# The room of the split weights holds four more expert tiles: a ring of eleven, and the turn of twice the slots at place 20

## The chip, the cores and the metric

One Trainium2 chip, and one of its cores. The metric is the device time of one execution in microseconds (us). The kernel before takes 2090.07 us, the median of three runs.

## The reference

Two transformer-like blocks on 256 tokens of width 1024, in f32. What matters here is the feed-forward part of the first block, a mixture of 32 experts:

```
logits = xt @ w_router + b_router
top_val, top_idx = lax.top_k(logits, 4)          # 4 of 32 experts for each of 256 tokens
hcat = xb @ w_in[e] + b_in[e]                    # 1024 -> 2048
act  = min(hcat[:, :1024], 7) * sigmoid(1.702 * .) * (clip(hcat[:, 1024:]) + 1)
y    = act @ w_out[e] + b_out[e]                 # 1024 -> 1024, added to the token by its gate
```

Ahead of it, in the first block, come the projections and two kinds of attention (the last four heads of the second kind are called "d" below) and a modulation vector that is made from the matrix `ada_w`. Behind it comes a second block: a retention part, convolutions, a state-space part and two more feed-forward parts.

## The kernel before

All large weights come from HBM as tiles of [128 x 2048] f32 (1 MB; those of `ada_w` are 0.5 MB) through one queue, that of SyncE (SP). The class `Stream` keeps the list of their sources in the order of use. `issue` asks for the next tile as long as the tile whose buffer it takes has been used; `ahead` asks for one tile out of turn, into a pool that is named.

The list begins with nine tiles of the projections (0 to 8) and four of the attention's output (9 to 12). From 13 on there are 12 for each of the 32 turns of the experts: eight of `w_in` and four of `w_out`; the first two turns interleave them, so that 13 to 28 are the `w_in` of turns 0 and 1 and 29 to 32 the `w_out` of turn 0. The experts end with tile 396.

In the other parts of the kernel a weight is not used as it comes. `Parts` splits each half of a tile in two numbers of fewer bits, `hi` (ScalarE, L141) and `lo` (VectorE, L142), and TensorE multiplies by both. Their buffers are the pool `wsplit`: four of `hi` and four of `lo`, 32 KB of each partition. The weights of the experts are not split, so `wsplit` holds nothing from the last projection to the end of the experts.

The ring of the tiles is `wst` (four buffers) with `mw` (three more), which exists while the experts run: seven tiles from tile 25 on. Tiles 13 to 24 are asked for during the attention, into `wst`, `mw` and two other pools (`hw`, `hx`).

Turns 0 and 1 have a fixed expert each. The later turns take their experts by the number of tokens, from a table `turn` that VectorE makes once the router is done; SP reads a turn's expert from it (TENSOR_LOAD, L1917) before it asks for the turn's tiles. An expert's tokens are gathered into slots: 64 for a turn, and 128 for the one turn `WIDE`, which takes the expert with the most tokens. For a 64-slot turn the two column halves of a product lie in the two row halves of one bank, and the profile shows the matmuls as 128*64; for the wide turn each half has a bank of its own and 128 rows, shown as 128*128 (`products`, L918). Gather is L900, transposes of the activations L947, scatter L1007.

On the engines the instructions stand in the order that a scheduler has given them; SP's queue is served in the order of issue.

Of the kernel before, what the change touches and what calls it, by code (L numbers as in the profile page):

```python
# [8 lines left out]
F32 = mybir.dt.float32  # L9
F32R = mybir.dt.float32r  # L10
# [8 lines left out]
NSTAGE = 4  # L19
# [18 lines left out]
AHEAD = 2  # L38
# [2 lines left out]


FIXED = 2
WIDE = 4
SLOTS = 64
S5W = 2816
INV2PI = 0.15915494309189535
# [19 lines left out]
class Stream:  # L67
# [2 lines left out]

    def __init__(self, nc, pool, n, width, late=None):
        self.nc, self.pool, self.n, self.width, self.late = nc, pool, n, width, late
        self.sources, self.tiles, self.more = [], {}, None
        self.issued = self.at = 0
        self.held = {}

    def add(self, srcs):
        self.sources += srcs

    def extend(self, pool, n, first, last):  # L80

        self.more = (pool, n, first, last)

    def ahead(self, i, pool):

# [3 lines left out]
    def issue(self, done):  # L89

        while self.issued < len(self.sources):
            i, pool, n = self.issued, self.pool, self.n
            if i in self.tiles:
                self.issued += 1
                continue
            if self.more and self.more[2] <= i < self.more[3] and (i - self.more[2]) % (self.n + self.more[1]) >= self.n:
                pool, n = self.more[:2]
            held = self.held.setdefault(id(pool), [])
            if len(held) >= n and held[-n] >= done:
                break  # L100
            held.append(i)
            self.load(i, pool.tile([128, self.width], F32, tag="w", name="w"))
            self.issued += 1
# [8 lines left out]
    def get(self):  # L112
        self.issue(self.at)
        self.at += 1
        return self.tiles.pop(self.at - 1)


class Parts:
# [7 lines left out]
    def get(self):  # L126
        st = self.stream
        end = 2 * len(st.sources)
        while self.ready < min(self.at + AHEAD + 1, end):
            i, h = divmod(self.ready, 2)  # L130
            if h == 0:
                st.issue(i)
                self.raw = st.tiles.pop(i)
            w = self.raw[:, h * 1024:(h + 1) * 1024]
            if self.ready in self.whole:
                self.made[self.ready] = (w,)
                self.ready += 1
                continue
            hi = self.pool.tile([128, 1024], F32R, tag="hi", name="hi")
            lo = self.pool.tile([128, 1024], F32R, tag="lo", name="lo")  # L140
            self.nc.scalar.copy(out=hi, in_=w)  # L141
            self.nc.vector.tensor_tensor(out=lo, in0=w, in1=hi.bitcast(F32), op=ALU.subtract)  # L142
            self.made[self.ready] = (hi, lo)
            self.ready += 1
        st.issue(self.ready // 2)
        self.at += 1
        return self.made.pop(self.at - 1)
# [146 lines left out]
def attention_block(tc, g):  # L294

    nc, A, ws = tc.nc, g.A, g.ws
    v, s, pe = nc.vector, nc.scalar, nc.tensor
    xT1 = g.xT1
    with ExitStack() as es:
# [135 lines left out]
        slots = [0, len(todo)]  # L435

        def ada_step(n=1):

            slots[0] += n
            for _ in range(min(len(todo) - slots[1] + slots[1] * slots[0] // ADA_PLACES, len(todo))):  # L440
                with tc.high_priority(offset=-LOW1):
                    todo.pop(0).step((lambda: bank1("s")) if todo else None)
# [79 lines left out]
        def stage_scores(heads, i):  # L522
            kind, c, j = heads[i]
            out = []
            for qt in range(2):
                qs = slice(qt * 128, (qt + 1) * 128)
                if kind == "g":
                    r = slice(64 * j, 64 * j + 64)
                    p, z = soft(scores(qT[r, c, qs], kaT[r, :], kind))
                    s.activation(out=p, in_=p, func=ACTF.Copy, scale=z)  # L530
                else:
                    pz = []
                    for m in range(2):
                        pz.append(soft(scores(qd[:, c, m, qs], kbT[:, c], kind)))
                    (p, z), (p1, z1) = pz
                    v.tensor_tensor(out=z1, in0=z1, in1=nlam, op=ALU.mult)
                    v.tensor_scalar(out=p, in0=p, scalar1=z, scalar2=None, op0=ALU.mult)
                    v.scalar_tensor_tensor(out=p, in0=p1, scalar=z1, in1=p, op0=ALU.mult, op1=ALU.add)
                out.append(p)
            pend[i] = out  # L540

        def stage_T(heads, i):
            pT = at.tile([128, 4, 256], F32, tag="pTs", name="pTs")
            for qt, p in enumerate(pend[i]):
                transposed(p, pT, qt)
            pend[i] = pT

        def stage_pv(heads, i):
            kind, c, j = heads[i]
            pT = pend.pop(i)  # L550
            o = bank1("o" if kind == "g" or c % 2 == 0 else "sc")
            if kind == "g":

                for k in range(4):
                    pe.matmul(out=o[:64, :256], lhsT=va[:, k, 64 * j:64 * j + 64], rhs=pT[:, k], start=(k == 0), stop=(k == 3))
                r = slice(64 * j, 64 * j + 64)
                s.copy(out=mix[r, c], in_=o[:64, :256])
            else:
                for k in range(4):
                    pe.matmul(out=o[:, :256], lhsT=vd[:, k, 128 * c:128 * c + 128], rhs=pT[:, k], start=(k == 0), stop=(k == 3))  # L560
                o2, osb = (o24[:, c % 2, j] for j in range(2))
                s.activation(out=o2, in_=o[:, :256], func=ACTF.Square)
                s.activation(out=osb, in_=o[:, :256], func=ACTF.Copy, scale=g.subln)
                for t in range(2):
                    pe.matmul(out=o[:, 256 + t:257 + t], lhsT=o2[:, t * 128:(t + 1) * 128], rhs=g.ones[:, :1], start=True, stop=True)
                r = rsqrt(nc, at, o[:, 256:258], 2, 1.0 / 128, "d", v)
                spread(g, at, r, o[:, 256:])
                v.tensor_tensor(out=mix[:, 4 + c], in0=osb, in1=o[:, 256:], op=ALU.mult)

        def attend(heads):  # L570
            n = len(heads)
            for i in range(n + 2):
                if i < n:
                    stage_scores(heads, i)
                if 0 <= i - 1 < n:
                    stage_T(heads, i - 1)
                if 0 <= i - 2 < n:
                    stage_pv(heads, i - 2)
                ada_step(2 if i % 2 else 1)
# [84 lines left out]
        for i in range(20, 24, 2):  # L664
            t = g.hw.tile([128, 2, 2048], F32, tag="h", name="hw")
            for j in range(2):
                ws.stream.load(i + j, t[:, j])
        attend([("d", h, 0) for h in range(4)])
        for i in (17, 18, 24):
            ws.stream.ahead(i, g.mw)  # L670
        ws.stream.extend(g.mw, 3, 25, 13 + 32 * 12 - 1)
        es_a.close()
        o1 = es.enter_context(tc.tile_pool(name="o1", bufs=1))
        sq, xs = (o1.tile([128, 8, 256], F32, name=n) for n in ("sq1", "xs"))
# [17 lines left out]
        first = pe.matmul(out=acc[:, :66], lhsT=g.ones[:1], rhs=g.zero, start=True, stop=False)  # L692
# [15 lines left out]
        last = tc.keep_in_program_order(chunk(7))  # L708
# [72 lines left out]
def turns(tc, g, mp, rp):  # L781
# [12 lines left out]
    jk = rp.tile([128, 32], F32, name="jk")  # L794
    v.tensor_scalar(out=jk, in0=g.iota[:, :32], scalar1=-1.0, scalar2=float(WIDE), op0=ALU.mult, op1=ALU.add)
    v.tensor_tensor(out=jk, in0=jk, in1=oh, op=ALU.mult)
    v.tensor_tensor(out=jk, in0=jk, in1=g.iota[:, :32], op=ALU.add)
    v.tensor_copy(out=jk[:, WIDE:WIDE + 1], in_=fx[:, 0:1])
    g.turn = mp.tile([128, 32], I32, name="turn")
# [3 lines left out]
    for t in range(2):  # L803
        for src, dst in ((g.rk, g.rkt), (g.gate, g.gatet)):
            sx = rp.tile([128, 1], F32, tag="sx", name="sx")
            v.scalar_tensor_tensor(out=jk, in0=src[:, t], scalar=1.0, in1=oh, op0=ALU.mult, op1=ALU.mult, accum_out=sx)
            v.scalar_tensor_tensor(out=jk, in0=src[:, t], scalar=src[:, t, WIDE:WIDE + 1], in1=oh, op0=ALU.subtract, op1=ALU.mult)
            v.tensor_tensor(out=dst[:, t], in0=src[:, t], in1=jk, op=ALU.subtract)
            v.tensor_copy(out=dst[:, t, WIDE:WIDE + 1], in_=sx)


def turn_biases(tc, g, rp):
# [6 lines left out]
    v.tensor_reduce(out=binx, in_=bx.rearrange("p e c -> p c e"), axis=AX.X, op=ALU.add)  # L819
    v.tensor_tensor(out=bx, in0=g.binT, in1=bc(g.binT[:, WIDE], 1, 32), op=ALU.subtract)  # L820
    v.tensor_tensor(out=bx, in0=bx, in1=bc(oh, 2, 16), op=ALU.mult)
    v.tensor_tensor(out=g.binT, in0=g.binT, in1=bx, op=ALU.subtract)
    v.tensor_copy(out=g.binT[:, WIDE], in_=binx)

# [1287 lines left out]
```

## Time and profile before

| | before |
|---|---|
| median of 3 runs | 2090.07 us (2088.04 to 2090.89) |
| the profiled execution | 2090.91 us, span 2089.2 us |
| TensorE busy | 1951.1 us, 93% |
| VectorE, ScalarE busy | 54%, 31% |
| queue of the weights | 613.46 MB, 75.1% of the span on 16 DMA engines |
| tiles' issue to landing, `w_in` | 13.1 us (median) |
| tiles' issue to landing, `ffn_up` (second block) | 5.0 us (median) |

The share of a span is a mean over stages: TensorE is the busier engine in the whole, but the row of GB/s shows a long flat part in the middle. A profile's row of slices cuts the span in 40 equal pieces; a window is a stretch that one chooses. A busy TensorE can hold small waits, since the ends of its matmuls are modelled.

### The profile page before, as it was taken

To read this page: it belongs to the slowest core of one execution; us is meant where nothing else is said; L and a number is where in the kernel's file an instruction comes from. 1 tells how busy PE (TensorE), PEld (TensorE's weight loads), DVE (VectorE), ACT (ScalarE), POOL (GpSimd) and SP (SyncE) were. 2 spreads that over 40 slices of the span, in tenths; PEclk is the share of its full clock that TensorE was granted. 3 is DMA by queue.
4 is the path that set the end of the run, shared out by engine and by line. 5 is a ranking of instruction groups with operands and counts; after the bars stand their busy time and mean duration, and the time that the engine had idled before them with its cause. 6 is when DMAs were issued, how large, how long until landed. Compare 5 with 4: busy or idle time off the path is not lost. (4 is left out here: it accounts for less than half of the span.)

```text
span 2089.2 us, 29010 instructions
## 1 busy us (share of the span) xinstructions
PE 1951.1 (93%) x11166; PEld 1246.5 (60%) x11166; DVE 1125.1 (54%) x2378; ACT 648.0 (31%) x1135; POOL 59.2 (3%) x92
## 2 busy tenths in 40 slices
PE   6999989999999989999998997999999999899998
PEld 3856844444333333332333326888999999599998
DVE  5865765132222212221222127999898978768863
ACT  3464311000000000000000004446677645256542
POOL 0000000000000000000000000000001002100000
PEclk9999989999999999999999998999999999799999
DMA  8656559999999999999999994667857778655651
GB/s 315 223 162 221 207 224 365 405 379 375 421 421 421 421 421 420 422 421 421 421 421 421 421 414 160 228 221 273 301 213 249 271 286 296 211 186 192 223 182 61
DMA packets 101757, 643.40 MB, mean 308 GB/s; under 512 B 11584, under 2 KB 12880, under 8 KB 34288
## 3 DMA queue, kind: packets, MB, share of 16 engines
q1 hardware_dynamic: 94176, 613.46, 75.1%
q0 software_dynamic: 6624, 26.76, 3.8%
q8 instruction: 89, 1.46, 0.3%
q10 hardware_dynamic: 816, 1.30, 0.2%
q14 instruction: 52, 0.43, 0.1%
HBM read 626.79 MB, written 14.68 MB: 307 GB/s over the span
## 5 line engine op out<-in xcount | busy, mean ns | idle before, releaser
L918 PE MATMUL hc<-w,xe 128*64 128x512 f32 (+1 forms) x2008 | 476.1, 598 | 54.1 <-DMA w<-in_w_in_dram 54.0
L918 PEld LDWEIGHTS hc<-w,xe 128*64 128x64 f32 (+1 forms) x2008 | 142.4, 138 | 375.3 <-issue 218.4
L142 DVE TENSOR_TENSOR lo<-w,hi 128x1024 fp32r<-128x1024 f32 x238 | 289.1, 1219 | 75.0 <-ACT hi L141 74.0
L141 ACT CAST hi<-w 128x1024 fp32r<-128x1024 f32 x238 | 249.0, 1049 | 253.0 <-PE b L241 156.7
L240 PE MATMUL b<-h2h,hi 128*128 128x256 f32 x896 | 254.6, 285 | 10.7 <-ACT h2h L1729 9.1
L938 DVE COPY hs<-hc 128x512 f32<-128x512 f32 x33 | 22.8, 691 | 448.8 <-PE hc L918 448.8
L241 PE MATMUL b<-h2l,hi 128*128 128x256 f32 x896 | 254.5, 285 | 0.2
L242 PE MATMUL b<-h2h,lo 128*128 128x256 f32 x896 | 253.9, 284 | 0.0
L918 PE MATMUL yb<-w,hb 128*64 128x512 f32 (+1 forms) x1024 | 252.6, 604 | 0.5 <-DMA w<-in_w_out_dram 0.5
L240 PEld LDWEIGHTS b<-h2h,hi 128*128 128x128 f32 x896 | 169.8, 190 | 13.3 <-ACT h2h L1729 9.3
L241 PEld LDWEIGHTS b<-h2l,hi 128*128 128x128 f32 x896 | 169.7, 190 | 4.0 <-issue 1.1
L242 PEld LDWEIGHTS b<-h2h,lo 128*128 128x128 f32 x896 | 169.7, 190 | 0.4 <-issue 0.4
L936 ACT COPY hs<-hc 128x512 f32<-128x512 f32 x33 | 19.3, 585 | 464.2 <-PE hc L918 464.2
L918 PEld LDWEIGHTS yb<-w,hb 128*64 128x64 f32 (+1 forms) x1024 | 66.8, 137 | 127.5 <-issue 119.5
L192 DVE SCALAR_TENSOR_TENSOR acc<-w,c,acc 128x1024 f32<-128x1024 f32 x77 | 98.4, 1278 | 12.0 <-DMA w<-in_ada_w_dram 11.4
L240 PE MATMUL b<-ah,hi 128*128 128x256 f32 x352 | 100.3, 286 | 0.0
L242 PE MATMUL b<-ah,lo 128*128 128x256 f32 x352 | 99.9, 284 | 0.2 <-DVE lo L142 0.2
L241 PE MATMUL b<-al,hi 128*128 128x256 f32 x352 | 99.4, 283 | 0.0
L981 ACT COPY ys<-yb 64x512 f32<-64x512 f32 (+1 forms) x32 | 18.5, 578 | 243.1 <-PE yb L918 243.1
L900 PEld LDWEIGHTS gb<-S,h 128*128 128x128 f32 x544 | 66.7, 197 | 37.2 <-issue 25.8
L1009 DVE TENSOR_TENSOR yacc<-sc,yacc 128x512 f32<-128x512 f32 x68 | 46.7, 688 | 66.5 <-PE sc L1007 66.5
L900 PE MATMUL gb<-S,h 128*128 128x128 f32 (+1 forms) x544 | 74.9, 289 | 1.2 <-DVE S L891 1.2
(523 smaller groups left out, 3061.1 us busy)
## 6 DMA issues: line engine op xcount, KB each, us to landing
w<-in_w_in_dram SPq DMA_DIRECT2D x252, 1024.0 KB, 13.1
w<-in_w_out_dram SPq DMA_DIRECT2D x128, 1024.0 KB, 14.5
w<-in_ffn_up_dram SPq DMA_DIRECT2D x44, 1024.0 KB, 5.0
w<-in_ada_w_dram SPq DMA_DIRECT2D x72, 512.0 KB, 5.0
w<-in_ret_w_in_dram SPq DMA_DIRECT2D x24, 1024.0 KB, 5.1
w<-in_ffn_down_dram SPq DMA_DIRECT2D x22, 1024.0 KB, 5.1
w<-in_w_ada_dram SPq DMA_DIRECT2D x32, 512.0 KB, 4.5
w<-in_ada_w_dram POOLq DMA_DIRECT2D x24, 512.0 KB, 4.8
```

The costliest lines, as they stand in the source:

```text
L141: self.nc.scalar.copy(out=hi, in_=w)
L142: self.nc.vector.tensor_tensor(out=lo, in0=w, in1=hi.bitcast(F32), op=ALU.subtract)
L192: v.scalar_tensor_tensor(out=self.acc, in0=w, scalar=cc, in1=self.acc, op0=ALU.mult, op1=ALU.add)
L240: pe.matmul(out=o, lhsT=w[0][:, sl], rhs=a[0][:, k], start=first, stop=False)
L241: pe.matmul(out=o, lhsT=w[0][:, sl], rhs=a[1][:, k], start=False, stop=False)
L242: pe.matmul(out=o, lhsT=w[1][:, sl], rhs=a[0][:, k], start=False, stop=last)
L900: g.got = pe.matmul(out=b[:, k * 128:k * 128 + n], lhsT=g.h2[:, t, d * 128:(d + 1) * 128], rhs=S[:, t, :n], start=(t == 0), stop=(t == 1))
L918: g.got = pe.matmul(out=on, lhsT=x, rhs=w[:, n * 512:n * 512 + 512], start=first, stop=last)
L936: s.copy(out=h, in_=hc[e][n])
L938: v.tensor_copy(out=h, in_=hc[e][n])
L981: s.copy(out=o, in_=i)
L1009: v.tensor_tensor(out=y, in0=b, in1=y, op=ALU.add)
```

## The change

`wsplit` has one kind of buffer instead of two: four of the size of a tile. For a split half `hi` is its first half and `lo` its second; the pool takes as much room as before. Between the projections and the end of the experts these four buffers hold tiles of the experts. Tiles 25 to 28 are asked for into them with `ahead`, before the "d" heads; from tile 29 on, the ring is `wst` (4), `mw` (3, until tile 395) and `wsplit` (4, until tile 389), eleven in all. The wide turn is at place 20 instead of 4.

```diff
-WIDE = 4
+WIDE = 20
...
-        self.sources, self.tiles, self.more = [], {}, None
+        self.sources, self.tiles, self.home = [], {}, {}
...
-    def extend(self, pool, n, first, last):
-
-        self.more = (pool, n, first, last)
+    def ring(self, first, slots):
+
+        k = 0
+        for i in range(first, len(self.sources)):
+            while k < len(slots) and slots[k][2] < i:
+                k += 1
+            if k == len(slots):
+                break
+            self.home[i] = slots[k][:2]
+            slots.append(slots[k])
+            k += 1
...
-            if self.more and self.more[2] <= i < self.more[3] and (i - self.more[2]) % (self.n + self.more[1]) >= self.n:
-                pool, n = self.more[:2]
+            pool, n = self.home.get(i, (self.pool, self.n))
...
-            hi = self.pool.tile([128, 1024], F32R, tag="hi", name="hi")
-            lo = self.pool.tile([128, 1024], F32R, tag="lo", name="lo")
+            parts = self.pool.tile([128, self.stream.width], F32, tag="w", name="parts").bitcast(F32R)
+            hi, lo = parts[:, :1024], parts[:, 1024:]
...
             t = g.hw.tile([128, 2, 2048], F32, tag="h", name="hw")
             for j in range(2):
                 ws.stream.load(i + j, t[:, j])
+
+        for i in range(25, 25 + AHEAD + 2):
+            ws.stream.ahead(i, ws.pool)
         attend([("d", h, 0) for h in range(4)])
         for i in (17, 18, 24):
             ws.stream.ahead(i, g.mw)
-        ws.stream.extend(g.mw, 3, 25, 13 + 32 * 12 - 1)
+        end = 13 + 32 * 12
+        wst, mw, wsp = (ws.stream.pool, NSTAGE, len(ws.stream.sources)), (g.mw, 3, end - 2), (ws.pool, AHEAD + 2, end - 8)
+        ws.stream.ring(25 + AHEAD + 2, [wst] * NSTAGE + [mw] * 3 + [wsp] * (AHEAD + 2))
```

(`AHEAD` is 2, so `AHEAD + 2` is the four buffers that `wsplit` has.)

**SP's queue in the attention.** The queue of SP just ahead of the "d" heads; `hw` and the `w_in` tiles are experts' weights, `ada_w` the modulation's. Before:

```order
L109 DMA w_1489<-in_w_o_dram 128x2048 [waits DVE_49]
L109 DMA w_1457<-in_ada_w_dram 128x1024 [waits DMAHW2_49,DVE_49]
L109 DMA hw_1573<-in_w_in_dram 128x2048 [waits DMAHW6_49,PE_49]
L109 DMA hw_1573<-in_w_in_dram 128x2048
L109 DMA hw_1576<-in_w_in_dram 128x2048 [waits PE_49]
L109 DMA hw_1576<-in_w_in_dram 128x2048
L109 DMA w_1460<-in_ada_w_dram 128x1024 [waits DMAHW3_49,DVE_49]
L109 DMA w_1503<-in_ada_w_dram 128x1024 [waits DMAHW5_49,DVE_49]
L109 DMA w_1954<-in_w_in_dram 128x2048 [waits DMAHW4_49,PE_49]
```

The same place of SP's queue in the changed kernel:

```order
L116 DMA w_1471<-in_w_o_dram 128x2048 [waits DVE_49]
L116 DMA w_1561<-in_w_in_dram 128x2048 [waits PE_49]
L116 DMA w_1563<-in_w_in_dram 128x2048 [waits DMAHW6_49,PE_49]
L116 DMA hw_1555<-in_w_in_dram 128x2048 [waits PE_49]
L116 DMA hw_1555<-in_w_in_dram 128x2048
L116 DMA hw_1558<-in_w_in_dram 128x2048 [waits PE_49]
L116 DMA hw_1558<-in_w_in_dram 128x2048 [waits DMAHW2_49]
L116 DMA w_1565<-in_w_in_dram 128x2048 [waits DMAHW3_49]
L116 DMA w_1567<-in_w_in_dram 128x2048 [waits DMAHW4_49]
L116 DMA w_1441<-in_ada_w_dram 128x1024 [waits DMAHW5_49,DVE_49]
L116 DMA w_1444<-in_ada_w_dram 128x1024 [waits DMAHW6_49,DVE_49]
L116 DMA w_1944<-in_w_in_dram 128x2048 [waits DMAHW7_49,PE_49]
```

The four new tiles stand around the four of `hw`, and the next tiles of `ada_w` behind all eight; the one `ada_w` tile that stood ahead of `hw` is now behind them too.

**SP's queue at the start of the experts.** The queue of SP right behind the first seven readings of the table. Before:

```order
L109 DMA w<-in_w_in_dram 128x2048 x5
L109 DMA w<-in_w_out_dram 128x2048 x2
L1917 TENSOR_LOAD turn
L1917 ISA x2
L1917 TENSOR_LOAD turn
L1917 ISA x2
L1917 TENSOR_LOAD turn
L1917 ISA x2
L1917 TENSOR_LOAD turn
L1917 ISA x2
L109 DMA w<-in_w_out_dram 128x2048 x2
```

The changed kernel:

```order
L116 DMA w<-in_w_in_dram 128x2048
L116 DMA w<-in_w_out_dram 128x2048 x4
L116 ISA
L116 DMA w<-in_w_in_dram 128x2048
L116 ISA
L116 DMA w<-in_w_in_dram 128x2048
L1929 TENSOR_LOAD turn
```

Seven tiles again, each four places further on in the list: the `w_in` of turn 1 are there, so that the seven end with the first two `w_in` of turn 2 instead of the second `w_out` of turn 0.

**TensorE's queue at the wide turn.** The products with 128 rows, with what stands around them. Before, at place 4:

```order
L918 MATMUL hc<-w,xe 128x512 x32
L900 MATMUL gb<-S,h_2150 128x128 x7
L918 MATMUL yb<-w,hb 64x512 x12
L947 MATMUL hT<-ident,hs 128x128
L918 MATMUL yb<-w,hb 64x512 x4
L947 MATMUL hT<-ident,hs 128x128 x11
```

The changed kernel, at place 20:

```order
L930 MATMUL hc<-w,xe 128x512 x32
L912 MATMUL gb<-S,h_2140 128x128 x5
L930 MATMUL yb<-w,hb 64x512 x12
L959 MATMUL hT<-ident,hs 128x128 x4
L930 MATMUL yb<-w,hb 64x512 x4
L959 MATMUL hT<-ident,hs 128x128 x12
```

The wide turn has the same parts in the same order; what changes is that sixteen more turns of 64 slots stand ahead of it.

## Rows read from the trace of the kernel before

**Rows 1.** The page: the span, and GB/s in 40 slices of it.

```profile
span 2089.2 us, 29010 instructions
...
GB/s 315 223 162 221 207 224 365 405 379 375 421 421 421 421 421 420 422 421 421 421 421 421 421 414 160 228 221 273 301 213 249 271 286 296 211 186 192 223 182 61
```

**Rows 2.** Busy time by windows: the experts' steady part, the second block.

```profile
core 0: us, PE busy (x) PEld busy (x) DVE busy (x) ACT busy (x) POOL busy (x), PEclk, DMA share, GB/s
540.00:1240.00 700.00, 641.77 (x2904) 222.68 (x2906) 166.14 (x326) 53.55 (x95) 0.00 (x0) 1.00 1.01 421
1262.00:2080.00 818.00, 787.24 (x5890) 734.32 (x5889) 669.85 (x1283) 438.82 (x741) 48.52 (x74) 0.97 0.63 223
```

**Rows 3.** TensorE's waits in 540:1252 (us in total, times, longest).

```profile
PE hc L918 <- DMA w<-in_w_in_dram: 53.5, 97, 1.3
```

**Rows 4.** SP's queue, 288:332 (start, length, instructions; waits lie between issues).

```profile
288.89 5.96 SPq L109 DMA_DIRECT2D w<-in_w_in_dram  x5
295.76 23.86 SPq L109 DMA_DIRECT2D w<-in_w_out_dram  x4
```

**Rows 5.** SP's waits in 288:1252.

```profile
SPq L109 <- PE hc L918: 401.1, 251, 17.5
```

**Rows 6.** Windows of 25 us, the columns of rows 2.

```profile
200.00:225.00 25.00, 24.99 (x112) 16.93 (x111) 24.34 (x81) 16.33 (x41) 0.00 (x0) 1.00 0.29 100
...
300.00:325.00 25.00, 24.99 (x109) 9.93 (x104) 10.76 (x42) 9.02 (x16) 0.55 (x1) 0.93 0.59 224
...
375.00:400.00 25.00, 24.63 (x103) 9.81 (x100) 8.19 (x16) 2.75 (x5) 0.00 (x0) 1.00 1.01 420
400.00:425.00 25.00, 25.00 (x72) 11.88 (x72) 1.84 (x3) 1.17 (x2) 0.00 (x0) 1.00 0.94 355
425.00:450.00 25.00, 24.65 (x116) 8.57 (x113) 8.92 (x23) 2.80 (x5) 0.00 (x0) 1.00 0.94 372
450.00:475.00 25.00, 24.80 (x78) 10.14 (x78) 7.55 (x12) 1.22 (x2) 0.00 (x0) 1.00 0.93 381
475.00:500.00 25.00, 24.79 (x118) 10.19 (x116) 8.84 (x20) 2.17 (x4) 0.00 (x0) 1.00 0.95 371
500.00:525.00 25.00, 24.80 (x130) 10.54 (x126) 4.72 (x8) 2.38 (x4) 0.00 (x0) 1.00 1.01 413
```

**Rows 7.** TensorE's timeline, 378:535: the wide turn's products and those of others.

```profile
378.22 1.94 PE L918 MATMUL hc<-w,xe 128*64 128x512 f32 x8 [0.17 <-DMA w<-in_w_in_dram]
...
395.31 27.63 PE L918 MATMUL hc<-w,xe 128*128 128x512 f32 x64
...
451.11 13.90 PE L918 MATMUL yb<-w,hb 128*128 128x512 f32 x32
...
468.57 7.09 PE L918 MATMUL hc<-w,xe 128*64 128x512 f32 x32
...
500.08 13.90 PE L918 MATMUL hc<-w,xe 128*64 128x512 f32 x64
```

**Rows 8.** SP's queue in the attention, 180:216.

```profile
182.12 0.33 SPq L109 DMA_DIRECT2D w<-in_ada_w_dram  x1
187.67 2.03 SPq L109 DMA_DIRECT2D hw<-in_w_in_dram  x4
191.03 2.80 SPq L109 DMA_DIRECT2D w<-in_ada_w_dram  x2
214.45 0.33 SPq L109 DMA_DIRECT2D w<-in_w_in_dram  x1
```

**Rows 9.** VectorE's timeline in the attention: first and last sums over `ada_w` tiles.

```profile
220.44 1.28 DVE L192 SCALAR_TENSOR_TENSOR acc<-w,c,acc 128x1024 f32<-128x1024 f32 x1
...
239.45 0.75 DVE L190 TENSOR_SCALAR acc<-w,c 128x1024 f32<-128x1024 f32 x1 [0.97 <-DMA w<-in_ada_w_dram]
```

**Rows 10.** The page's costliest groups (busy, mean ns, idle before): the split, and a product that waits for it.

```profile
L142 DVE TENSOR_TENSOR lo<-w,hi 128x1024 fp32r<-128x1024 f32 x238 | 289.1, 1219 | 75.0 <-ACT hi L141 74.0
...
L242 PE MATMUL b<-ah,lo 128*128 128x256 f32 x352 | 99.9, 284 | 0.2 <-DVE lo L142 0.2
```

More of the change, by code (lines that the diff above doesn't have):

```diff
@@ L91, in issue @@
         while self.issued < len(self.sources):
-            i, pool, n = self.issued, self.pool, self.n
+            i = self.issued
             if i in self.tiles:
```

## The prediction

> **What bounds the kernel now.** I read the page first, for the stages. Its row of GB/s [rows 1] has a flat piece of 421 from about 520 to 1200 us of the span; no other piece is that high or that even. That is the middle of the experts. The windows then say which engine waits there. From 540 to 1240 us the DMA engines are busy throughout (share 1.01) at 421 GB/s, while TensorE is busy 641.8 of 700 us [rows 2], and the table of TensorE's waits gives it 53.5 us in 97 waits for a `w_in` tile that has not landed [rows 3]. In this stage the queue of tiles is the bound and TensorE keeps up: its idle 700 - 641.8 = 58.2 us are its slack. A tile of 1.0486 MB takes 1.0486 MB / 421 GB/s = 2.49 us, a turn of twelve 29.9 us, and TensorE's slack is 58.2 x 29.9 / 700 = 2.5 us in each turn, at least, since a busy TensorE can hide small waits. The second block is another matter: from 1262 to 2080 us TensorE is busy 787.2 of 818 us at 223 GB/s [rows 2]. What the change does there must show in TensorE's queue, and what it does in the experts must show in the DMA's.
>
> So in the experts the time is the number of tiles still to bring, by 2.49 us, plus every microsecond in which the queue moves less than it could. I looked for those in windows of 25 us. There are two places. **Early:** at the start SP asks for seven tiles at 288.89 and 295.76 and then waits for a free buffer; the longest of its waits for a product of TensorE is 17.5 us, and the windows show 224 GB/s from 300 to 325 [rows 4 to 6]. TensorE is busy all of that window: it is working off what was loaded before, and sets the pace. **At the wide turn:** the queue is at 420 GB/s from 375 to 400, then 355, 372, 381, 371, 413, and after that it is flat [rows 6]. TensorE's timeline shows why. The 64 matmuls of the wide turn's up products take 27.63 us where another turn's take 13.90, and its 32 of down 13.90 instead of 7.09 [rows 7]. That is 20.5 us more on TensorE, while the queue brings tiles at its own pace until all seven buffers are full; then it can only go on as TensorE frees them, at 27.63 / 8 = 3.45 us a tile instead of 2.49.
>
> **The change part by part.**
>
> 1. *Four tiles loaded ahead.* They come during the "d" heads, where the DMA share is 0.29 [rows 6], into buffers that hold nothing then. At the start of the experts SP asks for seven more tiles as before, but each stands four places further on; after that each issue waits for the same products of TensorE, which frees buffers at the same times as long as it sets the pace. So the lead of four tiles is carried to the point where the queue becomes the bound, and there four fewer are left: 4 x 2.49 = **-9.96 us**. The wait of 17.5 us does not go away, and need not. Bounds: nothing, if the lead were lost before the queue is the bound; more than four tiles is not possible.
>
>    A rule bears on the price of a tile. The Trainium skill, "SBUF — State Buffer", section "The DMA setup-cost knee", says that each transfer pays about 2 us besides its bytes at 436 GB/s; by its formula a tile would take 4.4 us and the head start would be worth 17.6 us, as an estimate. The trace doesn't show that cost: at 421 GB/s with tiles queued behind one another [rows 2] the fixed part is hidden, so 2.49 us stands in the sum.
>
> 2. *The wide turn and the ring.* The loss there is counted against 421: (66 + 49 + 40 + 50 + 8) = 213, x 25 / 421 = 12.65 us. At 378.22, just ahead of the wide turn, TensorE waits 0.17 us for a tile [rows 7], so it had caught up, and the ring was empty of landed tiles, as it is at place 20. A ring with four more buffers lets the queue go on for four more tiles, 9.96 us, before it stops. I take the remaining loss as 12.65 - 9.96 = 2.7 us: **-9.96 us**. By the move alone I take nothing, since TensorE had caught up at place 4 as well; at place 20 it has had sixteen turns of slack of 2.5 us, which can only make the remaining loss smaller. Bounds: no loss (-12.65) to a loss of 5 us (-7.65, twice what is left), if gather and scatter of the neighbouring turns fall differently.
>
> 3. *After the wide turn.* TensorE has fallen behind by the 20.5 us above, and by some 4 to 5 more that I estimate for a gather of its own (32 small matmuls of 0.28 us are half shared in other turns) and its scatter: about 25 - 2.7 = 22 us. Eleven turns are left, with 11 x 2.5 = 27 us of slack. It catches up before the end, barely by this count; zero, with a bound of +5 us.
>
> 4. *The attention.* In SP's queue the four new tiles stand around the four of `hw`, and the `ada_w` tiles behind all eight. Before, one `ada_w` tile was asked for at 182.12, `hw` at 187.67, the next two `ada_w` at 191.03 and then nothing until 214.45 [rows 8]. Eight tiles from 187.67 take 8 x 2.49 = 19.9 us, to 207.6; the two `ada_w` tiles of half the size are in by about 211 to 213. VectorE sums over the first tile of this later group at 220.44 [rows 9], so they are some 7 us early. One sum of 1.28 us moves from ahead of the "d" heads to behind their start; VectorE is at 24.34 of 25 us there [rows 6], so it makes room in the one place and takes it in the other. I take 0, with bounds of -2 (VectorE's chain gets the sum off its way) and +2 us (the last sums wait for tiles already at 239.45, 0.97 us [rows 9], and one more tile has to come late).
>
> 5. *One buffer for `hi` and `lo`.* The split's subtraction takes 1.22 us and TensorE's product waits for `lo` 0.2 us in 352 [rows 10]: the split runs ahead, and four halves ahead remain allowed. A cast now also waits until the last of the products with `lo` is done. Hidden by the lead: 0, with a bound of 3 us to either side for the scheduler's small shifts in the second block.
>
> Sum: -9.96 - 9.96 + 0 + 0 + 0 = -19.9 us. Against the profiled execution of 2090.91 that is 2071.0; the median of the runs is 0.84 us less, so I say **2070 us**.
>
> **The rivals.**
>
> - *A, the ada tiles come late.* If the hw tiles start later than 187.67, because the two new ones ahead of them wait for TensorE to let go of the split buffers, the 7 us are gone, and the attention and all behind it slip by up to four tiles' time, 9.96 us: 2080. For it: SP's queue is served in order. Against: the 7 us, and that 27 us lie between 187.67 and the next tile at 214.45. (The Trainium skill, "SBUF — State Buffer", section "Can I just issue two DMAs to hit both halves?", says that all DMAs of a kernel land on the same 16 engines and serialize; by that rule another queue would not help, and the four tiles cost the others their full time. No row here sets two such queues side by side.)
> - *B, only the head start.* If the wide turn stops the queue as at place 4, for a reason other than the number of buffers (SP waiting behind one tile while others are free), only part 1 is left: 2080. Against: SP's waits name TensorE's products, that is buffers [rows 5].
> - *C, the other side.* With `hi` and `lo` in one buffer a cast waits for one product more, 0.284 us each [rows 10]. Over the 238 halves that is up to 68 us if all of it reached TensorE, and the gain is used up from 19.9 / 238 = 0.08 us per half on. Against: the lead of the split; TensorE waited 0.2 us in all for `lo`. The place to look is TensorE's idle time in the second block, 31 us before.
> - *D, no change.* The lead is used up before the queue is the bound, and the wide turn's loss at place 20 is not caught up (part 3) and comes back at the end of the experts: 2086 to 2092.
>
> **How the numbers follow.** My forecast 0.75, around 2070 with its own range 2065 to 2076 (the bounds of parts 2 to 5, not all on one side); A 0.07, B 0.08, both around 2080; C 0.05; D 0.05. Forecasts, A and B are all faster; the range of 2064 to 2081 takes in the forecast, A and B and leaves C, D and the mishaps of several parts out, about 1 in 10 to 2 in 10. A measurement of this kernel can tell about 0.2%, 4.2 us, from no change. Faster by more than that: 0.75 + 0.07 + 0.08 and a little of D, 0.91; within 0.2%: most of D, 0.05; slower: C, 0.04.
>
> **What would show it.** Part 1: the flat 421 GB/s begin as before and the last expert tile comes about 20 us earlier than before; the first experts' products start when they did. Part 2: no window under 415 GB/s from 400 to 525; instead a loss of 2 to 3 us at place 20, 16 turns x 29.9 = 478 us later, less the 20 us, near 860 us. Part 3: TensorE waits for tiles again before 1230. Part 4: the experts' first product within 2 us of its old time. Part 5: the second block as long as before within 3 us. I would be wrong if the dip at place 20 were as deep as at place 4, if the experts began late, or if TensorE's idle time in the second block grew.

## The result and the profile after

The changed kernel takes 2069.26 us (median of 4 runs, 2063.23 to 2072.28) against 2089.06 for the kernel before (4 runs): ratio 0.9899, 95% interval 0.9879 to 0.9919. The medians differ by 19.8 us; the ratio gives 21. In a later series, with more runs on both sides, it was 2068.7 against 2091.92, 0.9892 (0.9868 to 0.9915).

The profiled execution took 2072.28 us, with a span of 2070.6. Its page answers [rows 1]: the flat piece at 421 GB/s begins three slices earlier, since the dip ahead of it (365, 405, 379, 375) is gone, and it has one shallow notch (396) in its second half.

```profile
span 2070.6 us, 28975 instructions
...
GB/s 311 231 163 270 208 254 293 421 421 422 421 421 421 422 421 422 421 421 396 422 421 421 421 419 161 224 211 279 296 213 261 262 287 297 239 178 190 225 182 62
```

The windows show both places. They answer [rows 6]: columns are TensorE's busy time (and number of matmuls), weight loads, VectorE, ScalarE, GpSimd, granted clock (TensorE's clock as a share of its full speed), DMA share, GB/s.

```profile
300.00:325.00 25.00, 24.99 (x94) 9.24 (x92) 6.49 (x18) 6.51 (x10) 0.55 (x1) 0.80 0.50 203
...
400.00:425.00 25.00, 24.79 (x132) 10.52 (x128) 5.40 (x11) 1.80 (x3) 0.00 (x0) 1.00 1.01 421
...
450.00:475.00 25.00, 24.79 (x126) 10.10 (x126) 5.42 (x9) 2.38 (x4) 0.00 (x0) 1.00 1.01 421
475.00:500.00 25.00, 22.98 (x106) 7.70 (x106) 5.59 (x13) 2.01 (x4) 0.00 (x0) 1.00 1.01 420
...
925.00:950.00 25.00, 24.80 (x76) 10.08 (x75) 7.68 (x12) 1.80 (x3) 0.00 (x0) 1.00 0.99 410
950.00:975.00 25.00, 24.79 (x118) 10.19 (x116) 8.37 (x20) 2.17 (x4) 0.00 (x0) 1.00 0.98 401
975.00:1000.00 25.00, 24.79 (x128) 10.23 (x126) 5.20 (x9) 2.38 (x4) 0.00 (x0) 1.00 0.98 400
1000.00:1025.00 25.00, 24.79 (x114) 8.78 (x110) 8.16 (x19) 2.17 (x4) 0.00 (x0) 1.00 1.02 421
```

From 400 to 525 us the queue now runs at its full rate. The wide turn stands at 872 us, and the loss behind it is (11 + 20 + 21) x 25 / 421 = 3.1 us; it was 12.65. From 300 to 325 us the queue still stands half still. One thing here became important: TensorE is busy 24.79 of 25 us until 475, and only then begins to wait for tiles. Before, it had caught up by 378 [rows 7].

How long the experts take is read from the first start of their up products and the last start of their down products, in the view of one line (count, shortest/median/longest ns, first and last start). Changed kernel:

```profile
L930 PE MATMUL hc<-w,xe x2008: 592/592/644, 290.5 to 1217.4; 128*64 128x512 f32 x177, 128*128 128x512 f32 x6
L930 PE MATMUL yb<-w,hb x1024: 592/592/644, 334.9 to 1239.6; 128*64 128x512 f32 x166, 128*128 128x512 f32 x5
```

and the kernel before:

```profile
L918 PE MATMUL hc<-w,xe x2008: 592/592/644, 286.9 to 1232.7; 128*64 128x512 f32 x177, 128*128 128x512 f32 x6
L918 PE MATMUL yb<-w,hb x1024: 592/592/644, 328.1 to 1254.7; 128*64 128x512 f32 x166, 128*128 128x512 f32 x5
```

The experts take 1239.6 - 290.5 = 949.1 us against 1254.7 - 286.9 = 967.8: 18.7 us less. What lies ahead of them is 3.6 us longer, what lies behind (span less last start) 831.0 against 834.5, 3.5 us less. These two cancel, and the gain that is left is that of the experts. I call this stretch "the experts' time" below. It repeats within 1 us (949.1 and 949.2 in two profiles of the changed kernel, 966.4 and 966.8 in two of the kernel with the shared buffer alone), where the whole time of one kernel spreads over up to 19 us.

### The profile page after: what moved, and what is told of

Same layout as the page of the kernel before. It is cut to its first block, busy times and chain, and to the rows that moved or that the text cites. A ratio compares the mean times of both kernels' runs of the same rounds, so it can differ in the third digit from the quotient of the medians.

```text
span 2070.6 us, 28975 instructions
## 1 busy us (share of the span) xinstructions
PE 1942.3 (94%) x11166; PEld 1247.5 (60%) x11166; DVE 1126.4 (54%) x2378; ACT 649.9 (31%) x1135; POOL 59.3 (3%) x92
## 5 line engine op out<-in xcount | busy, mean ns | idle before, releaser
L930 PE MATMUL hc<-w,xe 128*64 128x512 f32 (+1 forms) x2008 | 470.9, 596 | 38.6 <-DMA w<-in_w_in_dram 38.2
L149 DVE TENSOR_TENSOR parts<-w,parts 128x1024 fp32r<-128x1024 f32 x238 | 289.8, 1221 | 64.9 <-ACT parts L148 63.5
L148 ACT CAST parts<-w 128x1024 fp32r<-128x1024 f32 x238 | 248.9, 1048 | 205.4 <-PE b L249 114.7
L247 PE MATMUL b<-h2h,parts 128*128 128x256 f32 x896 | 255.7, 286 | 10.3 <-ACT h2h L1741 9.1
L248 PE MATMUL b<-h2l,parts 128*128 128x256 f32 x896 | 255.6, 286 | 0.4 <-DVE h2l L1445 0.2
L249 PE MATMUL b<-h2h,parts 128*128 128x256 f32 x896 | 254.0, 284 | 0.0
L247 PEld LDWEIGHTS b<-h2h,parts 128*128 128x128 f32 x896 | 170.4, 191 | 12.7 <-ACT h2h L1741 9.3
L248 PEld LDWEIGHTS b<-h2l,parts 128*128 128x128 f32 x896 | 170.4, 190 | 4.2 <-issue 1.3
L249 PEld LDWEIGHTS b<-h2h,parts 128*128 128x128 f32 x896 | 170.2, 190 | 0.2 <-DVE al L1591 0.2
L247 PE MATMUL b<-ah,parts 128*128 128x256 f32 x352 | 100.5, 286 | 2.1 <-DVE xT L264 1.8
L249 PE MATMUL b<-ah,parts 128*128 128x256 f32 x352 | 99.9, 284 | 0.1
L248 PE MATMUL b<-al,parts 128*128 128x256 f32 x352 | 99.4, 283 | 0.0
L1543 PE MATMUL b<-parts,h2h 128*128 128x512 f32 x256 | 82.3, 401 | 0.9 <-DVE parts L149 0.6
## 6 DMA issues: line engine op xcount, KB each, us to landing
w<-in_w_in_dram SPq DMA_DIRECT2D x252, 1024.0 KB, 19.8
```

The source lines that it names most:

```text
L247: pe.matmul(out=o, lhsT=w[0][:, sl], rhs=a[0][:, k], start=first, stop=False)
L248: pe.matmul(out=o, lhsT=w[0][:, sl], rhs=a[1][:, k], start=False, stop=False)
L249: pe.matmul(out=o, lhsT=w[1][:, sl], rhs=a[0][:, k], start=False, stop=last)
L930: g.got = pe.matmul(out=on, lhsT=x, rhs=w[:, n * 512:n * 512 + 512], start=first, stop=last)
L1543: pe.matmul(out=bs[t], lhsT=x[:, kk, tsl], rhs=y[:, k * 512:(k + 1) * 512], start=(kk == 0 and i == 0), stop=(kk == 7 and i == 2))
```

## The experiments

Beside the shared buffer, which a fifth run has alone, the changed kernel does three things: it loads four tiles ahead, it makes the ring eleven deep, and it moves the wide turn. The first four runs take these apart.

**Ring and early tiles, wide turn at place 4.**

```diff
-WIDE = 20
+WIDE = 4
```

> The changed kernel with the wide turn back at place 4: early tiles and ring of eleven stay. Theory of the prediction (part 2): the move by itself is worth nothing, since TensorE had caught up at place 4 in the kernel before; about 2070 us, with a loss of some 3 us in the windows around 400. Rival: the four tiles of lead can be spent once only. With the lead, TensorE has not caught up at place 4 (in the changed kernel its waits for tiles begin only at about 475 us), the eleven buffers are already part full of landed tiles when the wide turn begins, and the queue loses its 12 to 13 us there as before: about 2079 us, and a hollow in GB/s from 400 to 525.

Measured: 2078.94 us (10 runs), 0.9958 (0.9935 to 0.9981) of the kernel before; the experts' time is 1245.6 - 286.3 = 959.3. The windows around the wide turn:

```profile
375.00:400.00 25.00, 24.79 (x113) 10.68 (x112) 9.54 (x21) 3.09 (x6) 0.00 (x0) 1.00 1.02 422
400.00:425.00 25.00, 25.00 (x62) 11.13 (x60) 0.72 (x2) 1.17 (x2) 0.00 (x0) 1.00 0.99 385
425.00:450.00 25.00, 24.65 (x124) 9.57 (x124) 9.92 (x23) 2.21 (x4) 0.00 (x0) 1.00 0.92 359
450.00:475.00 25.00, 24.80 (x78) 10.11 (x76) 7.67 (x12) 1.80 (x3) 0.00 (x0) 1.00 0.92 381
475.00:500.00 25.00, 24.79 (x120) 10.18 (x116) 8.15 (x19) 2.17 (x4) 0.00 (x0) 1.00 0.98 387
500.00:525.00 25.00, 24.79 (x127) 10.27 (x128) 5.42 (x9) 2.38 (x4) 0.00 (x0) 1.00 0.98 397
```

The hollow is back: (36 + 62 + 40 + 34 + 24) x 25 / 421 = 11.6 us, with eleven buffers. So the rival holds. TensorE is busy 24.79 of 25 us ahead of the wide turn, it has not caught up, and the buffers that would take up the wide turn's delay are in use already.

**The wide turn at place 20, ring of seven.**

```diff
-WIDE = 4
+WIDE = 20
```

(in the kernel before, nothing else)

> The kernel before with nothing but the wide turn moved to place 20: ring of seven. Both theories: a ring of seven loses its 12.65 us there as at place 4, so 2089 us and a hollow of that size near 870 to 1000 us. A third: at place 20 TensorE is further ahead and the loss is under 5 us; then 2080 us.

Measured: 2087.24 us (10 runs), 0.9992 (0.9973 to 1.0012); the experts' time is 1250.3 - 285.2 = 965.1. The windows there:

```profile
850.00:875.00 25.00, 23.14 (x102) 9.15 (x101) 8.20 (x16) 2.75 (x5) 0.00 (x0) 1.00 1.01 420
875.00:900.00 25.00, 25.00 (x60) 11.08 (x59) 0.69 (x1) 0.59 (x1) 0.00 (x0) 1.00 0.93 350
900.00:925.00 25.00, 24.65 (x121) 9.66 (x121) 10.13 (x23) 2.80 (x5) 0.00 (x0) 1.00 0.95 377
925.00:950.00 25.00, 24.80 (x76) 10.07 (x74) 7.67 (x12) 1.80 (x3) 0.00 (x0) 1.00 0.92 377
950.00:975.00 25.00, 24.79 (x119) 10.28 (x116) 8.15 (x19) 2.17 (x4) 0.00 (x0) 1.00 0.99 390
975.00:1000.00 25.00, 24.79 (x126) 10.14 (x126) 5.42 (x9) 2.38 (x4) 0.00 (x0) 1.00 0.98 398
```

The loss has moved with the turn: (1 + 71 + 44 + 44 + 31 + 23) x 25 / 421 = 12.7 us. With seven buffers the place is of little worth: nothing that the whole time can tell, and at most 2.7 us of the experts' time. (It is less against the two profiles of the shared buffer below, which have the wide turn at place 4 too and give 966.4 and 966.8.)

**Ring of eleven, nothing loaded ahead in the attention.**

```diff
-        for i in range(25, 25 + AHEAD + 2):
-            ws.stream.ahead(i, ws.pool)
...
-        ws.stream.ring(25 + AHEAD + 2, [wst] * NSTAGE + [mw] * 3 + [wsp] * (AHEAD + 2))
+        ws.stream.ring(25, [wst] * NSTAGE + [mw] * 3 + [wsp] * (AHEAD + 2))
```

> The changed kernel without the four tiles loaded ahead in the attention: the ring of eleven begins at tile 25, the wide turn is at place 20. Theory of the prediction (part 1): the head start is made by loading during the d heads, so without it only the gain at the wide turn is left: about 2079 us. Rival: the lead is the depth of the ring; the queue stood still from 309 to 323 us in the kernel before, and three or four tiles more fit into that gap: 2066 to 2070 us, and no window under 400 GB/s from 300 on. In either case the experts' first product comes 2 us earlier than in the changed kernel if it was the early tiles that delayed the attention.

Measured: 2066.04 us (4 runs), 0.9893 (0.9857 to 0.9928); the experts' time is 1232.4 - 284.9 = 947.5, 1.6 us under that of the changed kernel and 17.6 under seven buffers with the wide turn at the same place. Its windows:

```profile
300.00:325.00 25.00, 24.99 (x112) 10.70 (x112) 11.05 (x51) 9.54 (x17) 0.55 (x1) 0.93 0.73 289
325.00:350.00 25.00, 23.80 (x117) 8.96 (x117) 14.60 (x77) 2.97 (x6) 0.00 (x0) 1.00 1.01 422
```

The queue, which stood half still from 300 to 325 (224 GB/s before [rows 6]), goes on there at 289. The scheduler also puts one of the tiles (a `w_out` of turn 0) ahead of `hw` by itself, at 181.12 us. The lead comes without the early loading of the other three. The rival expected no window under 400 GB/s from 300 us on; the 289 fall short of that.

How large it is can be read at 400 us. The second run (seven buffers) and this one both have the wide turn at place 20, and their experts begin within 0.3 us of each other. The second run's windows, and this one's:

```profile
180.00:300.00 120.00, 107.19 (x544) 79.17 (x543) 83.56 (x295) 34.32 (x80) 4.93 (x4) 0.91 0.61 225
175.00:400.00 225.00, 209.94 (x1017) 121.13 (x1017) 126.05 (x452) 52.85 (x111) 5.48 (x5) 0.95 0.74 290
```

```profile
180.00:300.00 120.00, 107.30 (x545) 79.35 (x544) 83.08 (x295) 34.27 (x80) 4.92 (x4) 0.91 0.66 240
175.00:400.00 225.00, 210.54 (x1021) 121.77 (x1022) 126.03 (x452) 52.57 (x111) 5.48 (x5) 0.95 0.79 305
```

By 400 us the queue is (305 - 290) x 225 / 421 = 8.0 us of its full rate ahead, about three tiles. About half of that is there before 300 us, (240 - 225) x 120 / 421 = 4.3 us; the rest comes from 300 to 325, where seven buffers have 223 GB/s. With the smaller loss at the wide turn, 3.2 us against 12.7, that makes up the 17.6.

**Four tiles loaded ahead, but a ring of seven.**

```diff
-        ws.stream.ring(25 + AHEAD + 2, [wst] * NSTAGE + [mw] * 3 + [wsp] * (AHEAD + 2))
+        ws.stream.ring(25 + AHEAD + 2, [wst] * NSTAGE + [mw] * 3)
```

> The changed kernel with the four tiles loaded ahead, but their buffers not used again: from tile 29 on the ring has seven buffers; the wide turn is at place 20. Theory of the prediction, taken literally (four tiles fewer to bring): 2079 us. Rival (depth of the ring): tile 36 waits for tile 29 as in the kernel before, which holds it back to 330 us, so the lead shrinks to some 2 us by then, and the wide turn loses 12 to 13 us: 2086 to 2089 us.

Measured: 2104.09 us (6 runs), 1.007 (1.0043 to 1.0096): slower than the kernel before. The experts' time is 1258.9 - 288.1 = 970.8, 3.0 us more than before and 5.7 more than with seven buffers and the wide turn at the same place. Its windows:

```profile
300.00:325.00 25.00, 24.98 (x94) 9.09 (x92) 7.50 (x22) 6.51 (x10) 0.56 (x1) 0.80 0.48 182
325.00:350.00 25.00, 24.01 (x126) 10.52 (x124) 20.63 (x114) 6.52 (x12) 0.00 (x0) 1.00 0.61 232
```

The four tiles are there, and the queue stands still for as long as they save: 232 GB/s from 325 to 350, where the changed kernel has 384, is (384 - 232) x 25 / 421 = 9.0 us of queue time. Four fewer tiles to bring are worth nothing if the next ones may not be asked for earlier. The other 13 us of this run lie behind the experts (2106.3 - 1258.9 = 847.4 against 834.5 before), and neither theory had them; see the last section.

**The shared buffer alone.** The kernel before with one kind of buffer in `wsplit`:

```diff
-            hi = self.pool.tile([128, 1024], F32R, tag="hi", name="hi")
-            lo = self.pool.tile([128, 1024], F32R, tag="lo", name="lo")
+            parts = self.pool.tile([128, self.stream.width], F32, tag="w", name="parts").bitcast(F32R)
+            hi, lo = parts[:, :1024], parts[:, 1024:]
```

> The kernel before with nothing but the shared buffer of hi and lo; ring of seven, wide turn at place 4. Theory of the prediction (part 5): the split runs ahead, so no change, 2086 to 2092 us, and TensorE's waits for a split stay under 1 us in all. Rival C: casts that wait for one product more reach TensorE; slower by up to 60 us, with TensorE's idle time in the second block above 31 us.

Measured: 2085.06 us (10 runs), 0.9976 (0.9959 to 0.9993). Once more:

> The shared buffer of hi and lo alone, once more and in more rounds, beside the ring of nine. If the 5 us of the first look were the spread of the runs: 2087 to 2092 us, ratio within 0.2% of 1. If the shared buffer itself gives something: 2085 us again, 0.9976.

Measured: 2085.47 us (12 runs), 0.9988 (0.9967 to 1.0009). Rival C is out: casts that wait for one product more cost nothing. Whether the buffer gives 2 to 5 us stays open; the second interval holds 1. The experts' time is 1250.4 - 284.0 = 966.4 and 1250.8 - 284.0 = 966.8, so most of whatever there is lies elsewhere. TensorE waited 1.6 us in all for a split in the first run, somewhat more than the 1 us expected.

**The wide turn at place 28.**

```diff
-WIDE = 20
+WIDE = 28
```

> The changed kernel with the wide turn at place 28 instead of 20. Theory (part 3): TensorE falls some 22 us behind at the wide turn and makes good 2.5 to 3 us a turn, so that after three more turns and the last one's down some 10 to 14 us are left: 2079 to 2083 us, and TensorE doesn't wait for a tile again before the experts end. Rival: the queue is the bound to the end, and the place is of no matter: 2069 us.

Measured: 2080.42 us (10 runs), 0.9953 (0.9933 to 0.9972); the experts' time is 1254.2 - 293.8 = 960.4, 11.3 us more than at place 20. The time is as expected, and TensorE's waits for tiles after the wide turn are gone: three turns don't make good what the wide one costs. In the changed kernel they come back at about 1080 us, seven turns after the wide one begins.

**The changed kernel once more, and the ring without early tiles at place 12.** The second is the kernel of the third experiment with `WIDE = 12`.

> The changed kernel once more, beside the others: 2066 to 2072 us.

> The ring of eleven from tile 25 without the four tiles loaded ahead, and the wide turn at place 12. If a lead is spent once only and won back at 2.5 to 3 us a turn, any place will do at which TensorE has caught up and has turns enough left: the same as the changed kernel or up to 4 us less, 2065 to 2069 us, with a loss of under 4 us around the wide turn. Rival: sixteen turns ahead of the wide one are needed; then some of the 10 us come back, 2071 to 2076 us.

Measured: 2068.7 us (6 runs), 0.9892 (0.9868 to 0.9915), experts' time 1237.9 - 288.7 = 949.2; and 2065.79 us (5 runs), 0.9879 (0.9853 to 0.9905), experts' time 1235.3 - 284.9 = 950.4. Sixteen turns ahead of the wide one are not needed; with twelve the whole time is the same, and the experts' time 2.9 us longer than in the third experiment. This run has 220 GB/s from 300 to 325, no more than seven buffers; its lead (246 GB/s from 180 to 300 against 225, 6.0 us) is all there before 300 us.

**A ring of nine.** The third experiment's kernel with two of the four buffers in the ring (`[wsp] * 2`), wide turn at place 20. (The pool itself keeps its four buffers; nine is the number of places in the ring.)

> The ring from tile 25 without tiles loaded ahead, wide turn at place 20, but only two of the four buffers of the split in it: nine instead of eleven. If each buffer is spent twice (once as lead at the start, once at the wide turn), each is worth 2 x 2.49 = 4.98 us: half of the experts' gain, their first to last product about 958 us instead of 948 (eleven) and 968 (seven), 2074 to 2079 us in all. Rival: the gain hangs on a threshold (the lead must outlast the wide turn), and nine buffers give under a quarter of it: 2083 us or more, the experts 963 us or more.

Measured: 2071.97 us (6 runs), 0.9914 (0.9880 to 0.9948), under the 2074 to 2079 expected. The experts' time is 1245.1 - 285.1 = 960.0: 7.8 us under the kernel before, but 5.1 under seven buffers with the wide turn at the same place, where eleven give 17.6. The whole time fell by twice what the experts give; in the profile what lies behind the experts takes 826.6 us against 834.5, and why was not tried. Windows at the wide turn:

```profile
875.00:900.00 25.00, 25.00 (x60) 11.12 (x59) 0.69 (x1) 0.59 (x1) 0.00 (x0) 1.00 1.01 411
900.00:925.00 25.00, 24.65 (x120) 9.56 (x120) 10.13 (x23) 2.80 (x5) 0.00 (x0) 1.00 0.99 394
925.00:950.00 25.00, 24.80 (x76) 10.07 (x74) 7.67 (x12) 1.80 (x3) 0.00 (x0) 1.00 0.94 391
950.00:975.00 25.00, 24.79 (x120) 10.28 (x116) 8.15 (x19) 2.17 (x4) 0.00 (x0) 1.00 0.97 385
975.00:1000.00 25.00, 24.79 (x127) 10.14 (x126) 5.42 (x9) 2.38 (x4) 0.00 (x0) 1.00 1.00 404
```

The loss is (10 + 27 + 30 + 36 + 17) x 25 / 421 = 7.1 us. At place 20 it is 12.7 with seven buffers, 7.1 with nine, 3.1 with eleven: 2.8 and 2.0 us a buffer, about the 2.49 us that a tile takes. At the wide turn each buffer counts by itself.

The start is another matter. This run's windows there:

```profile
180.00:300.00 120.00, 106.56 (x556) 79.18 (x555) 85.14 (x297) 34.32 (x80) 4.93 (x4) 0.96 0.66 245
325.00:350.00 25.00, 22.55 (x114) 9.85 (x113) 19.06 (x107) 5.66 (x11) 0.00 (x0) 0.93 0.87 349
175.00:400.00 225.00, 208.55 (x1006) 120.53 (x1006) 127.60 (x454) 53.79 (x113) 5.48 (x5) 0.95 0.75 290
```

At 300 us the queue is as far ahead as with eleven places: (245 - 225) x 120 / 421 = 5.7 us. Then it falls back to 349 GB/s from 325 to 350, where seven buffers have 420 and eleven 422, and by 400 us it has moved no more than with seven (290 GB/s). So this ring does not keep the lead. Its buffers are spent once, at the wide turn (5.6 us less lost there, 5.1 less in the experts' time), and not twice as expected. Why two more places keep nothing of the lead where four keep it was not tried.

## Why the prediction was right, and where its steps were not

The time came out at 2069.26 for 2070, and the two terms of the sum have about their sizes: the experts give 18.7 us for 19.9. That the whole is closer still is luck: 3.6 us more ahead of the experts and 3.5 less behind them, neither foreseen, cancel. The reasons behind three of the steps did not hold.

1. **The head start (part 1).** The size holds roughly. The prediction has 9.96 us; the changed kernel's experts are 16.0 us under seven buffers at place 20, of which the wide turn gives 9.6 and the lead 6.4. Without early loading the lead is 8.0. That the wait "does not go away, and need not" holds too (203 GB/s from 300 to 325). The step that failed is that the four tiles loaded during the "d" heads are what makes the lead. Loading them without the deeper ring gave nothing (970.8), and the ring of eleven without them gave all of it (947.5), with one `w_out` tile put early by the scheduler. What the runs show in its place is that the ring must be deep enough to keep a lead once there. The ring of nine is 5.7 us ahead at 300 us and has lost it by 400, and the fourth run loses 9.0 us from 325 to 350; eleven places keep it. The bound "nothing, if the lead were lost before the queue is the bound" was the case of the fourth run.

2. **The wide turn (part 2).** The remaining loss was put at 2.7 us and is 3.1. The step that failed is "by the move alone I take nothing, since TensorE had caught up at place 4 as well". That is so in the kernel before, and there the move is indeed worth at most 2.7 us. With the lead it is not: TensorE catches up at about 475 us, and a wide turn at place 4 finds the buffers in use (11.6 us lost, experts 959.3). The four buffers are spent twice only if TensorE has caught up in between; so about 10 of the 19 us hang on the move. Ring and move together give 18.7, the move alone at most 2.7, the ring at place 4 (with the early tiles) 8.5: the remaining 7.5 or more are theirs together. With the place left at 4 the time would have been that of rival B (2078.94 for 2080), though not for B's reason.

3. **After the wide turn (part 3).** Held. It catches up by about 1080 us, seven turns, where 22 us at 2.5 us a turn would need nine. The estimate for the gather took 0.28 us for each small matmul; in a row sixteen take 2.05 us (from 870.53 in the changed kernel), so the gather's share is nearer to 2 us than to 4. The run at place 28 shows the price where it doesn't: 11.3 us.

4. **The attention (part 4).** Outside its bounds. The experts' first product came 3.6 us later. In the five profiles with early tiles it starts between 286.3 and 293.8 (mean 289.5), in the seven without between 284.0 and 286.9 (mean 285.0). The means differ by 4.5 us. Part of this lies ahead of `hw` already: SP asks for the last `w_o` tile at 182.46, before at 180.44. The step that failed is "it makes room in the one place and takes it in the other", put at 0. The `ada_w` tile that stood ahead of `hw` comes in the later group, which is five tiles over 12.52 us where it was four over 8.71, and VectorE's sum behind it waits 2.44 us for its tile where it waited 0.97 [rows 9]. First the kernel before, then the changed one:

```profile
221.75 8.71 SPq L109 DMA_DIRECT2D w<-in_ada_w_dram  x4
```

```profile
221.00 12.52 SPq L116 DMA_DIRECT2D w<-in_ada_w_dram  x5
243.97 0.75 DVE L197 TENSOR_SCALAR acc<-w,c 128x1024 f32<-128x1024 f32 x1 [2.44 <-DMA w<-in_ada_w_dram]
```

All five profiles with early tiles have the group of five over 12.52 or 12.53 us, all seven without it the group of four over 8.71. That the group makes the delay is read from these rows; no run moved that tile alone. This is rival A's direction with under half its price.

5. **The shared buffer (part 5).** Held for the buffer: zero or a few us of gain. The second block came out 3.5 us shorter, just outside the 3 us that were allowed.

Two of the signs of being wrong came in a small size: the experts began late (part 4), and TensorE's idle time in the second block grew from 30.8 us (818 - 787.24 [rows 2]) to 33.6 (814 - 780.42, from 1247 to 2061). The block was shorter all the same, so this sign told nothing of the time.

Rivals B and D did not come: the loss at the wide turn goes down with each buffer, and the lead is kept.

The version without early tiles, with the wide turn at place 12, is 3 us under the changed kernel in the same series (2065.79 against 2068.7; the intervals of their ratios overlap, so they are not told apart), with less code. I would take that one.

## What to carry to other kernels

A ring's depth is a budget in tiles, and how far ahead the queue may run is read from where the *next* transfer is allowed to be asked for, not from what has been loaded. If a stage begins with the consumer behind and has one slow step later, the same buffers pay for both, provided that the step stands far enough from the start for the consumer to have caught up, and far enough from the end to catch up again. A part of the buffers need not give its part of the gain: here nine places gave theirs at the slow step and none at the start. A stage's own length (first to last start of its products) tells such effects of 3 to 10 us where the kernel's whole time spreads by up to 19.

## What the runs showed of the hardware

With eleven buffers SP mostly waits for an earlier tile to land, and not for TensorE. SP's waits in 288:1252 of the changed kernel (total, times, longest), which answer [rows 5]:

```profile
SPq L116 <- DMA w<-in_w_in_dram: 299.2, 163, 2.9
SPq L116 <- DMA w<-in_w_out_dram: 173.4, 89, 6.9
SPq L116 <- PE hc L930: 153.6, 106, 20.2
SPq L116 <- PE yb L930: 103.1, 62, 5.1
```

That is 472.6 us for tiles against 256.7 for the experts' products. The queue stays full all the same (421 GB/s), so that costs nothing here.

What lies behind the experts, for the most part the second block, spreads over 20 us between the kernels though its work is nearly the same (826.6 to 847.4 us), and the mean granted clock of the whole profile falls as it grows: 0.982 with 827.0 us (the second run), 0.977 with 834.5 (the kernel before), 0.972 with 847.4. The slowest, the run with early tiles and seven buffers, in windows of 5 us:

```profile
1765.00:1770.00 5.00, 5.00 (x45) 5.00 (x44) 4.96 (x9) 2.53 (x4) 0.00 (x0) 1.00 1.02 418
1770.00:1775.00 5.00, 4.65 (x35) 3.61 (x34) 4.87 (x13) 4.87 (x8) 1.24 (x2) 1.00 1.01 412
1775.00:1780.00 5.00, 4.35 (x32) 4.25 (x31) 5.00 (x12) 1.19 (x3) 1.53 (x3) 0.81 0.61 211
1780.00:1785.00 5.00, 5.00 (x25) 5.00 (x25) 3.55 (x7) 0.40 (x1) 0.82 (x2) 0.50 0.88 319
...
1800.00:1805.00 5.00, 5.00 (x12) 1.84 (x12) 1.06 (x2) 0.00 (x0) 0.86 (x2) 0.50 0.93 339
1805.00:1810.00 5.00, 5.00 (x30) 3.22 (x29) 1.44 (x4) 1.32 (x3) 1.09 (x3) 0.96 0.70 233
```

After two short waits of TensorE (0.35 and 0.65 us) the clock falls to 0.50, that is 1.2 GHz, and stays there for some 27 us although TensorE is busy throughout; it does 25 matmuls in 5 us where it did 45 from 1765 to 1770. In the kernel before the same place has about 14 us at that level:

```profile
1780.00:1785.00 5.00, 3.34 (x4) 0.34 (x4) 4.21 (x9) 0.40 (x1) 0.33 (x1) 0.58 0.93 333
1785.00:1790.00 5.00, 5.00 (x23) 4.77 (x22) 0.00 (x0) 0.00 (x0) 0.56 (x1) 0.50 0.49 184
1790.00:1795.00 5.00, 5.00 (x14) 1.79 (x14) 3.21 (x7) 2.54 (x5) 1.62 (x3) 0.56 0.53 184
```

The 13 us more, at half speed, are an estimated 7 of the 13 us that this run is longer behind the experts. Why it falls for longer in this run was not tried.
